# Query and key latents of an attention layer: eight-piece blocks alternated over half their depth, with the loads of x and the first vector work re-ordered

## The chip, the cores and the metric

The kernel runs on one NeuronCore of a Trainium2 chip. The metric is the device time of one execution in microseconds (us). Lower is better. The engines are named as in the profile: PE (TensorE matmul), PEld (its weight loads), DVE (VectorE), ACT (ScalarE), POOL (GpSimd), SP (SyncE, which issues most transfers).

## The reference, cut to what matters

A trunk of two layers over 256 tokens of width 2048: an attention mixer with low-rank ("latent") projections, a dense MLP, a Mamba-2 mixer, a dense MLP, each behind an RMSNorm and added to the residual stream, all in float32. The change sits in the first few tens of microseconds, in the first lines of the attention mixer:

```
h = rms_norm(x, mix_norm_g[0])                       # (256, 2048)
a = h @ w_in                                         # 2048 x (512 + 512 + 64)
c_q, c_kv, k_rope = split(a, [512, 1024])            # "q" latent, "c" latent, "r"
q  = (rms_norm(c_q,  q_norm_g)  @ w_uq ).reshape(B, S, 16, 192)
kv = (rms_norm(c_kv, kv_norm_g) @ w_ukv).reshape(B, S, 16, 256)
```

## The kernel before, in words

**Three passes per matmul.** Every float32 product is made of three passes in a reduced format: weights w are split into a high part `wh` (a copy on ACT, L102) and a remainder `wl` (a subtraction on DVE, L103), and so are activations (high and low tiles `xt`). High by high, low by high and high by remainder are added in one PSUM bank `acc`, one bank for each 128 tokens (t = 0, 1).

**Units.** Weights come in units of 128 x 1024 floats: two depth steps (k) of 128 by 512 columns, 512 KB. A unit costs PE 12 matmuls of 512 columns: 8 on `wh` (L339 and L340), then 4 on `wl` (L343). The depth of 2048 is 16 steps, so the q latent takes 8 units (called q0 to q7 here), the c latent 8 units (c0 to c7). Between them stands the 64-column `r` block (`narrow_block`, L358) as one unit. `sequence` writes down the order of all units. `Flow` loads a unit's raw tile (`wraw`, 6 buffers) up to 6 units ahead of the block that PE is at, and splits it up to 3 ahead into `wh` and `wl`, of which there are 4 buffers each. The unit numbered n therefore writes into the buffer of unit n-4 and waits until PE has read that. The numbers in names such as `wh14` are unit numbers. In both kernels the first 13 units are twelve latent units and the `r` block, `wh13` to `wh16` are the last four c units (c4 to c7), and `wh17` and `wh18` the two units of the block that follows (`uq`, 384 columns).

**Activations.** x comes transposed (`xT`) in four tiles `k` of four depth steps each, in eight transfers of one, two or four steps. `split_x` makes the high part (ACT, L480; the first on DVE, L478) and the low part (DVE, L481). The norm's factor is not applied to x: it is taken from row sums of squares of a second copy of x (`stats`, ACT L296, issued by `X_AT`), becomes `rs` on POOL (L283, L428), and scales the finished latents.

**Between blocks.** `latent` takes a finished latent through its own norm: squares on ACT (L296, with `rs` as scale), sums on DVE (L282), a power on POOL (L283), a product with `rs` (L811) and two scaled products on DVE (L816). The results are transposed on PE (L324) and split again (L299, L300). `later(n, fn)` puts a piece of work off by n+1 calls of `tick`, and `block` calls `tick` once for each key, so twice two units. `fold` (L366) finishes the `r` block.

**What sets the order.** PE's instructions run as written. The other engines' instructions are put in order by a scheduler at build time, and each engine then runs its own list strictly in that order. SP has its issues in such a list, too, and a transfer is issued when an earlier one of eight has landed.

Of the kernel before, what the change touches and what calls it, by code (L numbers as in the profile page):

```python
# [45 lines left out]
def inv_two_pi_parts():  # L46
    from fractions import Fraction
    pi = Fraction(3141592653589793238462643383279502884197169399375105820974944592307816406286, 10 ** 75)
    rest, parts = 1 / (2 * pi), []
    for _ in range(5):  # L50
        e = math.floor(math.log2(float(rest)))
        step = Fraction(2) ** (e - 11)
        part = (rest / step).__floor__() * step
        parts.append(float(part))
        rest -= part
    return parts
# [90 lines left out]
def classical(key, src, nk=4, n=512):  # L147

    def units(flow):
        out = []  # L150
        if n == 64:
            ld = Load("raw", src)
            return [Unit(key, nk, n, [ld], lambda: flow.narrow_halves(ld.tile))]
        for k in range(0, nk, 2):
            ld = Load("raw", src[:, k * n:(k + 2) * n])
            first = key == ("ain", "q", 0)
            out.append(Unit(key, 2, n, [ld], lambda ld=ld, f=first: flow.halves(ld.tile, 2 * n, 512 if f else None)))
        return out
    return units


def part(key, src):

    def units(flow):
        ld = Load("raw", src)
        return [Unit(key, 2, 512, [ld], lambda: flow.halves(ld.tile, 1024))]
    return units


# [45 lines left out]
class Trunk:  # L215
# [109 lines left out]
        self.split_out(h, lo, b.rearrange("p (k n) -> p k n", k=4))  # L325


    def block(self, keys, lhs, n=512, accs=None, first=True, last=True, mid=None):
        nc = self.nc
        if accs is None:  # L330
            accs = [self.acc_tile() for _ in range(2)]
        kt = 0
        for ik, key in enumerate(keys):
            for nk, wh, wl, end in self.flow.piece(key):
                en = last and ik == len(keys) - 1 and end
                for q in range(nk):
                    for t in range(2):
                        ah, al = lhs(kt + q, t)
                        nc.tensor.matmul(accs[t][:, :n], ah, wh[:, q, :], start=first and kt + q == 0, stop=False)  # L339
                        nc.tensor.matmul(accs[t][:, :n], al, wh[:, q, :], start=False, stop=False)  # L340
                for q in range(nk):
                    for t in range(2):
                        nc.tensor.matmul(accs[t][:, :n], lhs(kt + q, t)[0], wl[:, q, :], start=False, stop=en and q == nk - 1)  # L343
                kt += nk
                if mid and not end:
                    mid()
            self.tick()
        return accs

    def narrow_block(self, key, tiles, then, lag=1):  # L350
# [88 lines left out]
    def start(self, seq):  # L439
        nc, d = self.nc, self.d  # L440
        self.flow = Flow(nc, self.wp, seq, (6, 3))
        cst = self.c.tile([P, C_END], F32, name="cst")
        self.cst = cst
        self.ident_r = self.c.tile([P, P], F32R, name="ident")
        self.ident = self.ident_r.bitcast(F32)
        self.mhalf = self.c.tile([P, 16], F32, name="mhalf")
        warm = self.s2.tile([P, 512], F32R, tag="s2", name="warm")
        nc.vector.memset(warm.bitcast(F32), 1.0)
        bank = self.sm.tile([P, 512], F32, tag="sm", name="warmed")
        for _ in range(WARM):  # L450
            nc.tensor.matmul(bank, warm[:, :P], warm, start=True, stop=True)
        nc.gpsimd.memset(self.mhalf, -0.5)
        nc.scalar.dma_start(cst[:, C_G0:C_GQ], d["cst"][:, C_G0:C_GQ])
        nc.scalar.activation(self.stat(1), self.mhalf[:, :1], AF.Copy)
        raws = [self.ktile(self.k4, F32) for _ in range(4)]
        parts = [(0, slice(k, k + 1)) for k in range(4)] + [(1, slice(0, 2)), (1, slice(2, 4)), (2, slice(0, 4)), (3, slice(0, 4))]

        def some_x():
            j, k = parts.pop(0)
            nc.sync.dma_start(raws[j][:, k], d["xT"][j][:, k])  # L460

        self.flow.load(2, ((0, 512), (512, 1024)), some_x)
        for u in range(3, 7):
            some_x()
            self.flow.load(u)
        self.pos = self.c.tile([P, 2], I32, name="pos")
        self.x = [[self.res.tile([P, 512], F32, name=f"x{t}{n}") for n in range(4)] for t in range(2)]

        self.rs_pool = [self.c.tile([P, 4], F32, name=f"rs{i}") for i in range(2)]
        self.phase = 0  # L470
        self.xT = [(self.ktile(self.xtp), self.ktile(self.xtp)) for _ in range(4)]

        def split_x(j, ks):
            h, lo = self.xT[j]
            for k in ks:
                g = cst[:, C_G0 + 4 * j + k:C_G0 + 4 * j + k + 1]
                if (j, k) == (0, 0):
                    nc.vector.tensor_scalar(h[:, k], raws[j][:, k], g, None, ALU.mult)  # L478
                else:
                    nc.scalar.activation(h[:, k], raws[j][:, k], AF.Copy, scale=g)  # L480
                nc.vector.scalar_tensor_tensor(lo[:, k], raws[j][:, k], g, h[:, k].bitcast(F32), ALU.mult, ALU.subtract)  # L481

        split_x(0, (0,))
        self.flow.convert(1)
        split_x(0, (1, 2))
        self.flow.convert(2)
        split_x(0, (3,))
        self.flow.load(7)
        one = self.scratch()
        nc.sync.dma_start(one[:, :P], d["one"])  # L490
        nc.gpsimd.tensor_copy(self.ident_r, one[:, :P])
        nc.sync.dma_start(cst[:, C_GQ:], d["cst"][:, C_GQ:])
        nc.sync.dma_start(self.pos, d["pos"])
        split_x(1, range(4))
        ssq = self.stat(8)
        self.later(0, lambda: split_x(2, range(4)))
        self.later(1, lambda: split_x(3, range(4)))

        def stats(n):
            for t in range(2):  # L500
                nc.sync.dma_start(self.x[t][n], d["x"][t * P:(t + 1) * P, n * 512:(n + 1) * 512])
                self.square_sum(self.x[t][n], ssq[:, t * 4 + n:t * 4 + n + 1])
            if n == 3:
                self.set_rstd(ssq)

        for n, at in enumerate(X_AT):
            self.later(at, lambda n=n: stats(n))
# [318 lines left out]
    def mla_body(self, mp, gain):  # L826
        nc, d = self.nc, self.d
        cq = [mp.tile([P, 4, 256], F32R, name=f"cq{i}") for i in range(2)]
        ckv = [mp.tile([P, 4, 256], F32R, name=f"ckv{i}") for i in range(2)]
# [5 lines left out]
            self.rope_tables(mp)  # L835

        self.later(2, setup)
        xT = self.from_tiles(self.xT)
        accs = self.block([("ain", "q", q) for q in range(4)], xT)
        for fn in self.latent(accs, d["qg"], cq):  # L840
            self.later(3, fn)

        kro = mp.tile([P, 2, 64], F32, name="kro")
        krss = mp.tile([P, 4], F32, name="krss")
# [10 lines left out]
                nc.vector.tensor_tensor(kro[:, t], kraw[:, t], self.cst[:, C_GK + 128:C_GK + 192], ALU.mult)  # L855
            nc.vector.tensor_scalar(krss, krss, EPS, None, ALU.add)

        self.narrow_block(("ain", "r", 0), self.xT, k_rope, 3)
        accs = self.block([("ain", "c", q) for q in range(4)], xT)
        lat = self.latent(accs, d["kvg"], ckv, False)  # L860
        self.rope(mp, kro.unsqueeze(2))

        gq = self.cst[:, C_GQ:C_GQ + HD]
# [140 lines left out]
        lhs = self.from_tiles(oT)  # L1004
# [387 lines left out]
                self.boundary_end()  # L1392


X_AT = (1, 2, 3, 3)
HEAD_BACKLOG = 4
SSM_ORDER = ["B0", "d0", "C0", "x0", "B1", "x1", "C1", "x2", "z0", "x3", "z1", "x4", "z2", "o0", "x5", "z3", "x6", "z4", "o1",
             "x7", "z5", "z6", "o2a", "z7", "o2b", "o3"]
# [72 lines left out]
def sequence(d):  # L1471
    seq = []
    add = lambda *a: seq.append(classical(*a))
    for q in range(4):
        add(("ain", "q", q), d["ain"][q, 0])
    add(("ain", "r", 0), d["ainr"], 16, 64)
    for q in range(4):
        add(("ain", "c", q), d["ain"][q, 1])
    uq = lambda u: add(("uq", u), d["uq"][u], 4, 384)
    ukv = lambda u: add(("ukv", u), d["ukv"][u])  # L1480
    wo = lambda nb, qs: [add(("wo", q, nb), d["wo"][q, nb]) for q in qs]
# [31 lines left out]
    for step in SSM_ORDER:  # L1513
        kind, i = step[0], int(step[1])
# [16 lines left out]
def trunk(tc, d, out):  # L1531
    with ExitStack() as ctx:
        ctx.enter_context(tc.manual_schedule(engines={mybir.EngineType.PE}))
        k = Trunk(tc, ctx, d, out)
        k.start(sequence(d))
        k.mla(d["g"][0])
        k.mlp(0, d["g"][1])
        k.ssm(d["g"][2])
        k.mlp(1, None)
        k.drain()  # L1540
# [67 lines left out]
```

## Time and profile before

| what | value |
|---|---|
| time, median of 3 runs | 2286.64 us (2286.34 to 2287.26) |
| profiled execution, first to last instruction (span) | 2284.5 us |
| profiled execution's own time outside the span | not given; the median is 2.1 us above the span |
| PE busy | 2278.1 us, 100% of the span |
| DVE / ACT / POOL busy | 1915.9 / 1390.1 / 275.5 us |
| mean DMA rate over the span | 244 GB/s |

Lines of the timeline read: start in us, length in us, engine, source line, operation, output<-input, shape, and in brackets the idle time before it and what ended that. SPq and ACTq are issuing slots. Ends of matmuls are modelled, so the spacing of their starts is the safer number.

### The profile page before, as it was taken

How to read it: one execution, taken by the hardware profiler on the slowest of the kernel's cores; microseconds unless marked ns; L12 is line 12 of the kernel's file. 1: busy time of each engine (PE TensorE's matmuls, PEld its weight loads, DVE VectorE, ACT ScalarE, POOL GpSimd, SP SyncE). 2: the span in 40 equal slices, each digit the busy share in tenths (PEclk: the TensorE clock that was granted, in tenths of full speed). 3: DMA queues.
4: the chain of work that ended last, by engine and by line, in shares of the span. 5: the costliest groups of instructions: out<-in, count | busy, mean ns of one | idle time of the engine just before them, and what ended most of it. 6: DMA issues, size and time to landing. Idle time of an engine off the chain costs nothing.

```text
span 2284.5 us, 30768 instructions
## 1 busy us (share of the span) xinstructions
PE 2278.1 (100%) x10929; PEld 1889.6 (83%) x10929; DVE 1915.9 (84%) x2318; ACT 1390.1 (61%) x1947; POOL 275.5 (12%) x315
## 2 busy tenths in 40 slices
PE   9999999999999999999999999999999999999999
PEld 7898888888888888888888888888888888888887
DVE  7786698999898897687899688676989889989985
ACT  7775576566666666564666555545666666666663
POOL 1440000000000000100133213121000000000000
PEclk9999999999999999999999999999999999999999
DMA  8545678888888878667888787767688888888874
GB/s 315 173 153 159 211 230 267 259 255 270 264 255 259 267 232 271 227 208 241 277 280 278 245 275 264 229 222 229 204 265 248 259 270 253 260 275 247 267 232 160
DMA packets 167706, 557.16 MB, mean 244 GB/s; under 512 B 19040, under 2 KB 28192, under 8 KB 166528
## 3 DMA queue, kind: packets, MB, share of 16 engines
q1 hardware_dynamic: 151264, 502.44, 66.2%
q0 software_dynamic: 13888, 48.49, 10.0%
q10 hardware_dynamic: 2400, 4.27, 0.5%
q8 instruction: 86, 1.41, 0.3%
q14 instruction: 68, 0.56, 0.1%
HBM read 529.65 MB, written 6.41 MB: 235 GB/s over the span
## 4 chain that ended last, share of the span: by engine, by line
PE 96%; DVE 1%; DMA 1%; ACT 1%; issue 1%; POOL 0%; SPq 0%; ACTq 0%; DVEq 0%
PE acc L339 13%; PE acc L340 13%; PE acc L343 13%; PE yp L618 9%; PE yp L617 9%; PE yp L616 9%; PE st L617 7%; PE st L618 7%; PE st L616 7%; DMA wraw<-mi 1%; PE sm L324 1%; DVE wl L103 1%; PE y L1309 1%; PE sm L322 1%; PE acc L616 1%; PE acc L618 1%
## 5 line engine op out<-in xcount | busy, mean ns | idle before, releaser
L102 ACT ACTIVATE wh<-wraw 128x1024 fp32r<-128x1024 f32 (+1 forms) x818 | 856.2, 1053 | 570.4 <-PE acc L340 268.9
L103 DVE TENSOR_TENSOR wl<-wraw,wh 128x1024 fp32r<-128x1024 f32 (+1 forms) x818 | 985.5, 1221 | 240.6 <-ACT wh L102 216.6
L616 PE MATMUL yp<-wh,k 128*128 128x512 f32 x896 | 349.2, 390 | 0.0
L618 PE MATMUL yp<-wh,k 128*128 128x512 f32 x896 | 348.8, 389 | 0.0
L617 PE MATMUL yp<-wl,k 128*128 128x512 f32 x896 | 348.6, 389 | 0.0
L339 PE MATMUL acc<-wh,xt 128*128 128x512 f32 x704 | 279.7, 397 | 0.4 <-ACT wh L102 0.4
L340 PE MATMUL acc<-wh,xt 128*128 128x512 f32 x704 | 274.9, 390 | 0.1
L102 ACT ACTIVATE wh<-wrx 128x1024 fp32r<-128x1024 f32 x168 | 177.8, 1058 | 153.4 <-PE yp L618 101.7
L103 DVE TENSOR_TENSOR wl<-wrx,wh 128x1024 fp32r<-128x1024 f32 x168 | 204.3, 1221 | 36.6 <-ACT wh L102 35.6
L618 PEld LDWEIGHTS yp<-wh,k 128*128 128x128 f32 x896 | 168.2, 188 | 35.1
L617 PEld LDWEIGHTS yp<-wl,k 128*128 128x128 f32 x896 | 168.2, 188 | 34.9
L616 PEld LDWEIGHTS yp<-wh,k 128*128 128x128 f32 x896 | 168.2, 188 | 34.8
L339 PE MATMUL acc<-wh,k 128*128 128x512 f32 x496 | 196.5, 396 | 0.0
L340 PE MATMUL acc<-wh,k 128*128 128x512 f32 x496 | 193.3, 390 | 0.0
L343 PE MATMUL acc<-wl,xt 128*128 128x512 f32 x704 | 188.3, 389 | 0.0
L616 PE MATMUL st<-wh,xt 128*128 128x512 f32 x448 | 177.7, 397 | 0.0
L618 PE MATMUL st<-wh,xt 128*128 128x512 f32 x448 | 174.9, 390 | 0.0
L617 PE MATMUL st<-wl,xt 128*128 128x512 f32 x448 | 174.7, 390 | 0.0
L339 PEld LDWEIGHTS acc<-wh,xt 128*128 128x128 f32 x704 | 132.7, 188 | 29.4 <-ACT wh L102 1.6
L340 PEld LDWEIGHTS acc<-wh,xt 128*128 128x128 f32 x704 | 132.5, 188 | 28.5 <-issue 1.2
L343 PEld LDWEIGHTS acc<-wl,xt 128*128 128x128 f32 x704 | 132.1, 188 | 27.7
L199 POOL DMA_DIRECT2D wrx<-mi x56 | 49.2, 878 | 720.6 <-DVE wl L103 524.5
(318 smaller groups left out, 3527.0 us busy)
## 6 DMA issues: line engine op xcount, KB each, us to landing
wraw<-mi SPq DMA_DIRECT2D x256, 512.0 KB, 5.5
wraw<-mo SPq DMA_DIRECT2D x256, 512.0 KB, 5.6
wraw<-si SPq DMA_DIRECT2D x160, 512.0 KB, 5.2
wraw<-so SPq DMA_DIRECT2D x64, 512.0 KB, 5.2
wrx<-mi SPq DMA_DIRECT2D x56, 512.0 KB, 5.4
wrx<-mi POOLq DMA_DIRECT2D x56, 512.0 KB, 7.8
wraw<-wo SPq DMA_DIRECT2D x32, 512.0 KB, 4.0
taps<-xD SPq DMA_DIRECT2D x16, 768.0 KB, 8.4
```

The costliest lines, as they stand in the source:

```text
L102: self.last = nc.scalar.activation(h[:, v], raw[:, v], AF.Copy)
L103: self.last_lo = nc.vector.tensor_tensor(lo[:, v], raw[:, v], h[:, v].bitcast(F32), ALU.subtract)
L199: nc.gpsimd.dma_start(st["b11"].tile, quarter(d, 1, 0), accum_op=ALU.add)
L322: self.nc.tensor.transpose(b.bitcast(F32R)[:, v], words[:, v], self.ident_r)
L324: self.nc.tensor.transpose(b[:, v], src[:, v], self.ident)
L339: nc.tensor.matmul(accs[t][:, :n], ah, wh[:, q, :], start=first and kt + q == 0, stop=False)
L340: nc.tensor.matmul(accs[t][:, :n], al, wh[:, q, :], start=False, stop=False)
L343: nc.tensor.matmul(accs[t][:, :n], lhs(kt + q, t)[0], wl[:, q, :], start=False, stop=en and q == nk - 1)
L616: nc.tensor.matmul(b, ah, wh, start=first and q == 0, stop=False)
L617: nc.tensor.matmul(b, ah, wl, start=False, stop=False)
L618: nc.tensor.matmul(b, al, wh, start=False, stop=last and q == 1)
L1309: nc.tensor.matmul(y[t][c, o], part(t)[:, c], xg[g][t][:, o], start=True, stop=True)
```

## The change: what it does

- The 16 latent units are put in a new order: q0 c0 q1 c1 q2 c2 q3 c3, then q4 to q7, then the `r` block, then c4 to c7. Both latents hold their PSUM banks (4 in all) from the start. `tick` is called once per two units of one latent.
- Since two latents share each x tile in the first half, x's tile 1 is loaded between weights, and tiles 2 and 3 after seven units of weights.
- Within a unit the two token halves alternate: high t0, high t1, low t0, low t1, where it was high t0, low t0, high t1, low t1.
- DVE's first instructions are put in written order: both first low parts of x before the first weight remainder `wl0`.
- The q latent's transposes are put off by 1 instead of 3, the `r` block's `fold` by 2 instead of 3, and `X_AT` moves the last piece of `stats` one tick on.

```diff
-            first = key == ("ain", "q", 0)
-            out.append(Unit(key, 2, n, [ld], lambda ld=ld, f=first: flow.halves(ld.tile, 2 * n, 512 if f else None)))
+            out.append(Unit(key, 2, n, [ld], lambda ld=ld: flow.halves(ld.tile, 2 * n)))
...
-def part(key, src):
+def part(key, src, step=None):
...
-        return [Unit(key, 2, 512, [ld], lambda: flow.halves(ld.tile, 1024))]
+        return [Unit(key, 2, 512, [ld], lambda: flow.halves(ld.tile, 1024, step))]
...
-    def block(self, keys, lhs, n=512, accs=None, first=True, last=True, mid=None):
+    def block(self, keys, lhs, n=512, accs=None, first=True, last=True, mid=None, tick=True):
...
-                    for t in range(2):
-                        ah, al = lhs(kt + q, t)
-                        nc.tensor.matmul(accs[t][:, :n], ah, wh[:, q, :], start=first and kt + q == 0, stop=False)
-                        nc.tensor.matmul(accs[t][:, :n], al, wh[:, q, :], start=False, stop=False)
+                    for part in range(2):
+                        for t in range(2):
+                            nc.tensor.matmul(accs[t][:, :n], lhs(kt + q, t)[part], wh[:, q, :],
+                                             start=first and kt + q + part == 0, stop=False)
...
-            self.tick()
+            if tick:
+                self.tick()
...
-        for u in range(3, 7):
+        for u in (4, 6):
+            self.flow.load(u)
             some_x()
-            self.flow.load(u)
...
-        split_x(0, (0,))
-        self.flow.convert(1)
-        split_x(0, (1, 2))
+        with self.tc.manual_schedule(engines={mybir.EngineType.DVE}):
+            split_x(0, (0, 1))
+            self.flow.convert(1)
         self.flow.convert(2)
-        split_x(0, (3,))
+        split_x(0, (2, 3))
         self.flow.load(7)
+        some_x()
+        some_x()
...
-        xT = self.from_tiles(self.xT)
-        accs = self.block([("ain", "q", q) for q in range(4)], xT)
-        for fn in self.latent(accs, d["qg"], cq):
-            self.later(3, fn)
+        lat = {n: [self.acc_tile() for _ in range(2)] for n in "qc"}
+
+        def latents(steps):
+            for n, i in steps:
+                self.block([("ain", n, i)], self.from_tiles(self.xT, 2 * i), accs=lat[n], first=i == 0, last=i == 7, tick=i % 2)
+
+        latents(LATENTS[:12])
+        for fn in self.latent(lat["q"], d["qg"], cq):
+            self.later(1, fn)
...
-        self.narrow_block(("ain", "r", 0), self.xT, k_rope, 3)
-        accs = self.block([("ain", "c", q) for q in range(4)], xT)
-        lat = self.latent(accs, d["kvg"], ckv, False)
+        self.narrow_block(("ain", "r", 0), self.xT, k_rope, 2)
+        latents(LATENTS[12:])
+        lat = self.latent(lat["c"], d["kvg"], ckv, False)
...
-X_AT = (1, 2, 3, 3)
+X_AT = (1, 2, 3, 4)
+LATENTS = [(n, i) for i in range(4) for n in "qc"] + [("q", i) for i in range(4, 8)] + [("c", i) for i in range(4, 8)]
```

Three places where the order of instructions moves. In the names, `wraw` and `wh` are raw and high weights, `k` the raw tiles of xT, `xt` split x, `acc_16` and `acc_17` the q latent's banks, `s2` scratch tiles, `cq` the transposed q latent.

SP's issues before, from the second half of the second unit (`wraw_124`) on. Names such as `k_3` are x tiles: `k_2` is x's first tile.

```order
L85 DMA wraw_124<-ain 128x512
L460 DMA k_2_115<-xT 128x256
L460 DMA k_3_116<-xT 128x512
L85 DMA wraw_130<-ain 128x1024
L460 DMA k_3_116<-xT 128x512
L85 DMA wraw_133<-ain 128x1024
L460 DMA k_4_117<-xT 128x1024
L85 DMA wraw_136<-ain 128x1024
L460 DMA k_5_118<-xT 128x1024
```

The same place in the changed kernel:

```order
L85 DMA wraw_124<-ain 128x512
L460 DMA k_2_115<-xT 128x256
L85 DMA wraw_129<-ain 128x1024
L85 DMA wraw_131<-ain 128x1024
L460 DMA k_3_116<-xT 128x512
L85 DMA wraw_134<-ain 128x1024
L85 DMA wraw_136<-ain 128x1024
L460 DMA k_3_116<-xT 128x512
L85 DMA wraw_181<-ain 128x1024
L460 DMA k_4_117<-xT 128x1024
L460 DMA k_5_118<-xT 128x1024
```

The third unit's weights moved ahead of a half of x's second tile; x's last two tiles (`k_4`, `k_5`) moved behind three and four more units.

ACT's list around the q latent's squares, before. `s2_31` and `s2_32` are the squares of `acc_16` and `acc_17`.

```order
L102 ACTIVATE wh14_545<-wraw14_464 128x1024
L102 ACTIVATE wh15_563<-wraw15_507 128x1024
L296 ACTIVATE s2_31_443,st_30_442<-acc_16_204,rs0_150 128x512
L296 ACTIVATE s2_32_445,st_30_442<-acc_17_205,rs0_150 128x512
L777 ACT_TABLE_LOAD
L777 ACTIVATE angp_361<-angs_360 128x64
L778 ACTIVATE angp_361<-angs_360 128x64
L102 ACTIVATE wh16_593<-wraw16_525 128x1024
L102 ACTIVATE wh17_611<-wraw17_543 128x768
L102 ACTIVATE wh18_659<-wraw18_561 128x768
L299 ACTIVATE cq0_199<-sm_43_627 128x4x128
```

And in the changed kernel, where the squares write `s2_33` and `s2_34`:

```order
L102 ACTIVATE wh16_596<-wraw16_483 128x1024
L102 ACTIVATE wh17_614<-wraw17_501 128x768
L102 ACTIVATE wh18_646<-wraw18_541 128x768
L295 ACTIVATE s2_33_520,st_32_519<-acc_16_207,rs0_148 128x512
L295 ACTIVATE s2_34_522,st_32_519<-acc_17_208,rs0_148 128x512
L298 ACTIVATE cq0_202<-sm_43_630 128x4x128
L298 ACTIVATE cq0_202<-yp_44_637 128x4x128
```

The squares moved from ahead of the splits `wh16` to `wh18` to behind them.

PE's list at the q latent's transposes, before: the end of unit `wh14`, the transposes, the fold, the next unit.

```order
L340 MATMUL acc_42_506<-wh14_545,xt_11_157 128x512
L343 MATMUL acc_41_505<-wl14_546,xt_10_156 128x512
L343 MATMUL acc_42_506<-wl14_546,xt_10_156 128x512
L343 MATMUL acc_41_505<-wl14_546,xt_10_156 128x512
L343 MATMUL acc_42_506<-wl14_546,xt_10_156 128x512
L324 MATMUL sm_43_627<-ident_97,s2_37_455 128x128 x4
L324 MATMUL yp_44_634<-ident_97,s2_38_457 128x128 x4
L366 MATMUL sm_45_641<-cst_96,s2_40_503 128x64 x2
L339 MATMUL acc_41_505<-wh15_563,xt_12_158 128x512
```

And in the changed kernel:

```order
L338 MATMUL acc_19_210<-wh14_503,xt_11_155 128x512
L342 MATMUL acc_18_209<-wl14_504,xt_10_154 128x512
L342 MATMUL acc_19_210<-wl14_504,xt_10_154 128x512
L342 MATMUL acc_18_209<-wl14_504,xt_10_154 128x512
L342 MATMUL acc_19_210<-wl14_504,xt_10_154 128x512
L323 MATMUL sm_43_630<-ident_97,s2_39_532 128x128 x4
L323 MATMUL yp_44_637<-ident_97,s2_40_534 128x128 x4
L338 MATMUL acc_18_209<-wh15_543,xt_12_156 128x512
```

The transposes stand behind the same unit in both; the fold moved from here to behind unit `wh16`. Between the q latent's last matmul and these transposes stood the `r` block and six c units before; now the `r` block and two.

More of the change, by code (lines that the diff above doesn't have):

```diff
@@ L1473, in sequence @@
     add = lambda *a: seq.append(classical(*a))
[L1474 to L1478, printed above, removed]
+    for j, (n, i) in enumerate(LATENTS):
+        if j == 12:
+            add(("ain", "r", 0), d["ainr"], 16, 64)
+        seq.append(part(("ain", n, i), d["ain"][i // 2, "qc".index(n)][:, (i % 2) * 1024:(i % 2) * 1024 + 1024], 512 if j < 2 else None))
     uq = lambda u: add(("uq", u), d["uq"][u], 4, 384)
```

## The prediction

> **What bounds the kernel.** I read the page's busy times and the chain first, then the stages of the first 100 us, then the timeline of each engine there.
>
> ```profile
> PE 2278.1 (100%) x10929; PEld 1889.6 (83%) x10929; DVE 1915.9 (84%) x2318; ACT 1390.1 (61%) x1947; POOL 275.5 (12%) x315
> PE 96%; DVE 1%; DMA 1%; ACT 1%; issue 1%; POOL 0%; SPq 0%; ACTq 0%; DVEq 0%
> core 0: 2284.5 us, clock 1.000
> ```
>
> PE idles for 2284.5 - 2278.1 = 6.4 us in all. A change that keeps PE's work can only remove part of that, or add to it. Behind the first 73 us the lists of all engines are the same in both kernels but for names and line numbers, so the early stretch decides. In the stages below the columns are length, then busy time and count for PE, PEld, DVE, ACT, POOL, then clock, DMA share and GB/s.
>
> ```profile
> 5.45:9.40 3.95, 3.81 (x13) 2.75 (x13) 3.02 (x7) 2.88 (x6) 0.00 (x0) 1.00 0.91 273
> 9.40:12.67 3.27, 2.90 (x13) 2.00 (x11) 1.86 (x5) 2.26 (x5) 0.00 (x0) 1.00 1.02 402
> 12.67:15.53 2.86, 2.86 (x12) 2.36 (x13) 2.86 (x4) 2.56 (x5) 0.00 (x0) 1.00 1.02 418
> ...
> 1.45 4.21 PE L451 MATMUL warmed<-warm 128*128 128x512 f32 x9 [1.45 <-DVE warm L448]
> 5.45 0.63 PE L339 MATMUL acc<-wh,xt 128*128 128x512 f32 x1
> 6.22 0.79 PE L340 MATMUL acc<-wh,xt 128*128 128x512 f32 x1
> 7.24 0.50 PE L340 MATMUL acc<-wh,xt 128*128 128x512 f32 x1
> 7.58 0.40 PE L339 MATMUL acc<-wh,xt 128*128 128x512 f32 x1
> 12.67 0.50 PE L339 MATMUL acc<-wh,xt 128*128 128x512 f32 x1 [0.37 <-ACT wh L102]
> 15.53 0.39 PE L339 MATMUL acc<-wh,xt 128*128 128x512 f32 x1
> 18.25 0.39 PE L339 MATMUL acc<-wh,xt 128*128 128x512 f32 x1
> ```
>
> A unit in step takes 18.25 - 15.53 = 2.72 us; the first three took 3.95, 3.27 and 2.86, so 1.92 us above three such units. In step, starts are 2.72/12 = 0.23 apart. Part of the excess is slow matmuls: the warm-up ones are (5.45 - 1.45)/9 = 0.44 apart, and from 7.24 to 7.58 it is still 0.34. Part is waiting: 0.77 from 5.45 to 6.22 (x's low part), and the wait before the third unit.
>
> **Start: alternating units, x later, remainder behind x.** PE's second matmul is now the other token half's high part, at about 5.45 + 0.44 = 5.89; the low part is needed third, at 6.33. DVE makes it right behind the first high part, so before 6.0:
>
> ```profile
> 5.08 0.68 DVE L103 TENSOR_TENSOR wl<-wraw,wh 128x512 fp32r<-128x512 f32 x1
> 5.69 0.48 DVE L481 SCALAR_TENSOR_TENSOR xt<-k,cst,xt 128x256 fp32r<-128x256 f32 x1
> 5.91 0.49 ACT L480 ACTIVATE xt<-k,cst 128x256 fp32r<-128x256 f32 x1
> 11.56 1.06 ACT L102 ACTIVATE wh<-wraw 128x1024 fp32r<-128x1024 f32 x1 [0.51 <-DMA wraw<-ain]
> 14.79 1.71 ACT L480 ACTIVATE xt<-k,cst 128x256 fp32r<-128x256 f32 x4 [0.22 <-DMA k<-xT]
> ```
>
> x's second step is ready on ACT at 6.40 and its low part near 6.95; both remainders follow by 6.95 + 2 x 0.68 = 8.31. PE needs the first of them eight starts behind 5.45: four at 0.44, one at 0.34, three at 0.23, or 8.24. So the first unit ends near 8.31 + 4 x 0.23 = 9.2, for 9.4 in the first row above. The second (c0) uses the same two steps of x, so it runs in step to 11.9, where before q1 needed x's third and fourth step. The third needs its weights, which landed at 11.54 with 256 KB of x ahead of them. At 402 GB/s those cost 0.65 us, so they land near 10.9 and are split by 11.95. The third unit starts at about 12.0 and the fourth at 14.73 for 15.53: **gain 0.8 us**. Bounds: nothing, if the weights land no sooner; 1.9, the whole excess. I take 0.8, which follows the rows. Moving x's tiles 2 and 3 back costs nothing: tile 2 was split at 14.79, and even four units of 512 KB more ahead of it are 4 x 1.3 = 5.2 us at 402 GB/s, while PE wants it at the ninth unit, 14.73 + 5 x 2.72 = 28.3. The pairing of token halves leaves the matmul count alone; zero.
>
> **The wait that is added.** The q latent's squares stand behind `wh18` on ACT. That split writes the buffer of `wh14`, so it waits until PE has read unit c5, and PE's next instructions after c5 are the transposes that need those squares. Before, the same split waited at the same place, with the squares long done:
>
> ```profile
> 41.41 0.67 ACT L296 ACTIVATE s<-acc,rs 128x512 f32<-128x512 f32 x1
> 48.60 0.85 ACT L102 ACTIVATE wh<-wraw 128x768 fp32r<-128x768 f32 x1 [1.82 <-PE acc L340]
> ...
> 48.18 0.39 PE L340 MATMUL acc<-wh,xt 128*128 128x512 f32 x1
> 48.41 1.07 PE L343 MATMUL acc<-wl,xt 128*128 128x512 f32 x4
> 49.32 0.60 PE L324 MATMUL sm<-ident,s 128*128 128x128 f32 x4
> 49.75 0.60 PE L324 MATMUL yp<-ident,s 128*128 128x128 f32 x4
> 50.19 0.56 PE L366 MATMUL sm<-cst,s 128*128 128x64 f32 x4
> 50.55 0.48 PE L339 MATMUL acc<-wh,xt 128*128 128x512 f32 x1
> ```
>
> Let H be the start of that split. PE would reach the transposes at H + 49.32 - 48.60 = H + 0.72 and, as the fold has left this place, the next unit at H + 50.19 - 48.60 = H + 1.59. The chain's price is read off the c latent, which has the same steps behind an equal split:
>
> ```profile
> 55.47 0.85 ACT L102 ACTIVATE wh<-wraw 128x768 fp32r<-128x768 f32 x1 [0.98 <-ACT s L296]
> 56.22 0.67 ACT L296 ACTIVATE s<-acc,rs 128x512 f32<-128x512 f32 x1
> ...
> 57.68 0.17 DVE L282 TENSOR_SCALAR st<-st 128x2 f32<-128x2 f32 x1 [0.34 <-ACT s L296]
> 57.93 0.72 POOL L283 TENSOR_TENSOR st<-st,mhalf 128x2 f32<-128x2 f32 x1 [3.11 <-DVE st L282]
> 58.69 0.16 DVE L811 TENSOR_TENSOR st<-st,rs 128x2 f32<-128x2 f32 x1 [0.84 <-POOL st L283]
> 58.88 1.41 DVE L816 SCALAR_TENSOR_TENSOR s<-acc,st,gb 128x512 f32<-128x512 f32 x2
> ```
>
> Split to squares 0.75; squares to the end of the first product 58.88 + 0.70 - 56.22 = 3.36, of the second 58.88 + 1.41 - 56.22 = 4.07. With 0.05 to PE (5.69 + 0.48 to 6.22), the transposes start at H + 4.16 and H + 4.87, and the next unit at 4.87 + 0.44 = H + 5.31. **Cost 5.31 - 1.59 = 3.7 us.** Bounds: 3.0, were the split free; about 5, if DVE, which has `wl18` (0.95) ahead of the sums, also delays them. That remainder is done near H + 1.9 and the squares near H + 2.2, so it should not. The factor `rs` is not what is late: before, it took from 37.81 to 40.37 + 0.53 = 40.90 from the last square of x to the factor, 3.1 us:
>
> ```profile
> 42.86 1.28 ACT L777 ACT_TABLE_LOAD   x1
> 37.81 0.62 ACT L296 ACTIVATE s<-x 128x512 f32<-128x512 f32 x1
> 40.37 0.53 POOL L428 COPY rs<-st 128x2 f32<-128x2 f32 x1
> ```
>
> The last two squares now stand behind `wh15`, whose buffer is read at 14.73 + 8 x 2.72 + 8 x 0.23 = 38.3, with the table load between them: 38.3 + 1.06 + 0.7 + 1.28 + 0.4 + 3.1, about 45, against H near 48.60 - 0.8 = 47.8. What is queued behind `wh18` are only these squares; DMA issues on SP go on, as raw buffers are freed by DVE's remainders of earlier units.
>
> **Behind it.** The fold (0.36) is moved, not removed: zero. It now opens the `uq` block, and its four small squares on ACT and POOL's rotation stand ahead of the c latent's chain, some 2 us; that chain had finished at 60.29, while PE reached its transposes at 62.40, so its 2.1 us of cover are about used up. Next comes PE's one wait there:
>
> ```profile
> 62.40 1.03 PE L324 MATMUL sm<-ident,s 128*128 128x128 f32 x8
> 67.78 1.39 POOL L798 TENSOR_TENSOR ra<-qn,cc 128x256 f32<-128x256 f32 x1 [4.08 <-DVE qn L887]
> 70.74 1.89 DVE L887 SCALAR_TENSOR_TENSOR qn<-yp,st,cst 128x128 f32<-128x128 f32 x8 [2.17 <-POOL st L290]
> 71.88 0.63 PE L939 MATMUL yp<-ident,qn 128*128 128x128 f32 x4 [0.41 <-DVE qn L887]
> ```
>
> The transposes need the `yp` bank that these products read. They wait for a root on POOL, which stood behind the rotation's first piece (1.39) before and now stands ahead of it; PE comes 0.36 later by the fold. That is 1.7 us in favour, for a wait of 0.41. So the 0.41 goes: **gain 0.4 us**, bounds 0.4 and -1, if the late c chain pushes the same products back.
>
> **Sum.** 3.7 - 0.8 - 0.4 = +2.5 us. The profiled span becomes 2287.0; what lies outside it (2.1 us to the median, which is all the runs tell of it) is untouched, so 2286.64 + 2.5 = 2289.1.
>
> **A rule that speaks against it.** PE stands still from H + 0.88 (48.41 + 1.07) to H + 4.16, 3.3 us, with only transposes until H + 5.31. No gap in this trace is that long, so no row shows whether PE's matmuls are slow again behind it, as they were up to 7.3 us. The Trainium skill, "TensorE: Matmul & The Clock Gate", "Part 1: The HAM clock gate", says an idle window of about 3.4 us halves PE's clock until a like window of work; one such slow window would add an estimated 3.4 x (1 - 0.23/0.44) = 1.6 us, giving 2290.7. The granted clock cannot settle it: the column reads 1.00 during the slow start too.
>
> **Rivals.**
> - *PE comes back slow (0.17).* From rows: slow starts ran from 1.45 to about 7.3, 5.8 us at 0.44 for 0.23, or 2.8 us lost. At most 2289.1 + 2.8 = 2291.9, at least a little over 2289.1. For it: the length of the stop. Against: 3.3 us is short of the 5.8 that the start took.
> - *No new wait, so faster (0.08).* If PE's stop at the transposes is under 1.2 us, the two gains decide; without any stop 2286.64 - 1.2 = 2285.4. That needs the squares to run while `wh18` waits. ACT's list speaks against it, and in the trace ACT's work behind such a split started only as it ended (55.47, then 56.22).
> - *The start gains nothing (0.10).* Weights land as late as before; then 2289.9. For it: DMA share is 1.02 throughout. Against: 256 KB less lie ahead.
> - *A second wait at the late c chain (0.12).* Up to 1 us more at the `uq` block's transposes and 0.4 not gained: 2290.5.
>
> **How the numbers follow.** The forecast holds 0.53. A change within 0.2% (4.57 us), about what a measurement here can tell from none, reaches to 2291.2. The slow return passes that in perhaps half of its cases, a double wait in some: slower 0.12. Nothing in 6.4 us of idle time makes 4.57 us likely: faster 0.01. The range takes in the start's bounds, the second wait and half of the slow return: 2287.6 to 2291.6.
>
> **What would show it.** Right: PE's idle time at L323's first transposes near 48.5 us, about 3.3 us, released by DVE L818; the fourth unit at about 14.7; no wait at the first `qn` transposes. Wrong: squares (L295 on `acc`) ahead of the last 768-column split's start, or matmuls 0.44 apart behind the stop.

## The result, and the profile after

The changed kernel took 2289.71 us (median of 21 runs, 2286.49 to 2291.14), the kernel before 2286.22 (21 runs, 2285.41 to 2288.19). The ratio is 1.0015, 95% interval 1.0009 to 1.0021: 3.5 us slower, within the 0.2% called no difference above. The profiled execution spans 2287.7 us, 3.2 more than before.

The page's busy times and the clock of the core, after:

```profile
PE 2278.2 (100%) x10929; PEld 1890.0 (83%) x10929; DVE 1916.4 (84%) x2318; ACT 1390.2 (61%) x1947; POOL 270.9 (12%) x315
core 0: 2287.7 us, clock 0.999
```

PE's count is the same. Its sum of busy time moved by 0.1 only, though matmuls ran slow for a while: 1.5 us more from the transposes to the end of c6's high products stand against 0.7 less up to the fourth unit, 0.4 less on the first `ckv` unit and some tenths elsewhere. The sum hides all of that; the starts show it. The timeline of PE after, in four stretches (high products are now L338, products with remainders L342, transposes L323; one row is a run of equal instructions):

```profile
4.97 1.17 PE L338 MATMUL acc<-wh,xt 128*128 128x512 f32 x4
8.79 2.09 PE L338 MATMUL acc<-wh,xt 128*128 128x512 f32 x8
12.02 2.11 PE L338 MATMUL acc<-wh,xt 128*128 128x512 f32 x8 [0.22 <-ACT wh L102]
14.87 1.30 PE L338 MATMUL acc<-wh,xt 128*128 128x512 f32 x5
...
47.74 1.07 PE L342 MATMUL acc<-wl,xt 128*128 128x512 f32 x4
52.26 1.08 PE L323 MATMUL sm<-ident,s 128*128 128x128 f32 x4 [3.45 <-DVE s L818]
53.14 1.06 PE L323 MATMUL yp<-ident,s 128*128 128x128 f32 x4
53.85 2.90 PE L338 MATMUL acc<-wh,xt 128*128 128x512 f32 x8
56.59 1.09 PE L342 MATMUL acc<-wl,xt 128*128 128x512 f32 x4
...
69.92 2.01 PE L338 MATMUL acc<-wh,ckv 128*128 128x512 f32 x8
72.68 1.98 PE L338 MATMUL acc<-wh,ckv 128*128 128x512 f32 x8
75.40 0.60 PE L946 MATMUL yp<-ident,qn 128*128 128x128 f32 x4
75.97 1.66 PE L338 MATMUL acc<-wh,cq 128*128 128x384 f32 x8
```

The answering rows of before that were not shown yet, from the same view of PE:

```profile
52.49 1.08 PE L343 MATMUL acc<-wl,xt 128*128 128x512 f32 x4
65.35 0.40 PE L339 MATMUL acc<-wh,ckv 128*128 128x512 f32 x1
65.81 0.50 PE L340 MATMUL acc<-wh,ckv 128*128 128x512 f32 x1
68.59 0.39 PE L339 MATMUL acc<-wh,ckv 128*128 128x512 f32 x1
72.48 0.42 PE L339 MATMUL acc<-wh,cq 128*128 128x384 f32 x1
```

PE runs its list in order, so the difference of starts between equal points is a ledger:

| stretch on PE | before | after | difference |
|---|---|---|---|
| to the start H of `wh18`'s split | 48.60 | 47.94 | -0.66 |
| H to the first matmul of unit c6 (before, the fold's 0.36, which both kernels pay once, is left out) | 1.59 | 5.91 | +4.32 |
| c6's eight high products | 1.94 | 2.74 | +0.80 |
| c6's low products to the first unit on `ckv` (before, with the fold's 0.36 put in) | 13.22 | 13.33 | +0.11 |
| first unit on `ckv` | 3.24 | 2.76 | -0.48 |
| second unit on `ckv` to the first `qn` transposes | 3.29 | 2.72 | -0.57 |
| sum | | | +3.52 |

At the next block's first product PE is 75.97 - 72.48 = 3.49 late; the medians differ by 3.49. That the two agree so closely is chance: behind this point single executions differ by more. The run e1 below stands 0.57 us ahead of the kernel before here (71.91), and its span is still 1.5 us longer (2286.0).

The stop is 3.45 us long and ended by DVE L818, the latent's scaled product. The chain ahead of it, from the timelines of ACT, DVE and POOL after:

```profile
47.94 0.85 ACT L102 ACTIVATE wh<-wraw 128x768 fp32r<-128x768 f32 x1 [1.82 <-PE acc L338]
48.70 0.67 ACT L295 ACTIVATE s<-acc,rs 128x512 f32<-128x512 f32 x1
50.16 0.17 DVE L281 TENSOR_SCALAR st<-st 128x2 f32<-128x2 f32 x1 [0.29 <-ACT s L295]
50.41 0.73 POOL L282 TENSOR_TENSOR st<-st,mhalf 128x2 f32<-128x2 f32 x1 [4.10 <-DVE st L281]
51.37 1.41 DVE L818 SCALAR_TENSOR_TENSOR s<-acc,st,gb 128x512 f32<-128x512 f32 x2
45.07 0.18 POOL L428 COPY rs<-st 128x2 f32<-128x2 f32 x1
```

ACT waits 1.82 us in front of `wh18` with the squares queued behind it. Their factor `rs` was there at 45.25, so it was the order of ACT's list and no late input that held them.

Behind the stop the matmuls are slow, and the windows of 1 us after (columns as above) show it in the granted clock, the third figure from the right:

```profile
51.00:52.00 1.00, 0.00 (x0) 0.00 (x0) 0.79 (x2) 0.00 (x0) 0.14 (x1) 1.00 0.83 215
52.00:53.00 1.00, 0.74 (x4) 0.77 (x5) 1.00 (x3) 0.00 (x0) 0.00 (x0) 0.59 0.37 148
53.00:54.00 1.00, 1.00 (x7) 1.00 (x5) 0.10 (x1) 0.60 (x1) 0.00 (x0) 0.50 0.41 49
54.00:55.00 1.00, 1.00 (x4) 0.81 (x4) 0.82 (x2) 0.60 (x1) 0.00 (x0) 0.50 0.64 211
55.00:56.00 1.00, 1.00 (x5) 0.81 (x4) 0.56 (x1) 0.00 (x0) 0.00 (x0) 0.71 0.08 16
56.00:57.00 1.00, 1.00 (x6) 0.83 (x5) 0.00 (x0) 0.21 (x1) 0.00 (x0) 1.00 0.01 2
```

If a reading of 0.59 means a part of the window at half, the time at half is 0.82 + 1 + 1 + 0.58 = 3.4 us. The core's mean clock, 0.999 against 1.000, is the same thing seen from far off: 3.4 x 0.5 of 2288 us is 0.07%. Of the 21 executions 17 read 0.999 (median 2290.27) and four 1.000 (2286.49 to 2288.86, median 2287.6). The 2.7 us between these medians are no price of the slow window: there are only four, and the executions of the kernel before lie 2.8 us apart by themselves. The mean clock is printed to 0.001, so a stretch at half clock of less than about 2.3 us (0.0005 x 2288 / 0.5) would still read 1.000.

### The profile page after: what moved, and what is told of

Its sections match the earlier page's. It is cut to its first block, busy times and chain, and to the rows that moved or that the text cites. A ratio compares the mean times of both kernels' runs of the same rounds, so it can differ in the third digit from the quotient of the medians.

```text
span 2287.7 us, 30764 instructions
## 1 busy us (share of the span) xinstructions
PE 2278.2 (100%) x10929; PEld 1890.0 (83%) x10929; DVE 1916.4 (84%) x2318; ACT 1390.2 (61%) x1947; POOL 270.9 (12%) x315
## 4 chain that ended last, share of the span: by engine, by line
PE 96%; DMA 1%; DVE 1%; ACT 1%; issue 0%; POOL 0%; SPq 0%; ACTq 0%; DVEq 0%
PE acc L338 26%; PE acc L342 13%; PE yp L618 9%; PE yp L619 9%; PE yp L620 9%; PE st L619 7%; PE st L620 7%; PE st L618 7%; PE sm L323 1%; PE y L1316 1%; PE sm L321 1%; PE acc L620 1%; PE acc L619 1%; PE acc L618 1%; DMA wraw<-mi 1%; DVE wl L103 0%
## 5 line engine op out<-in xcount | busy, mean ns | idle before, releaser
L338 PE MATMUL acc<-wh,xt 128*128 128x512 f32 x1408 | 355.0, 394 | 0.6 <-ACT xt L480 0.4
L338 PEld LDWEIGHTS acc<-wh,xt 128*128 128x128 f32 x1408 | 262.3, 188 | 58.1 <-issue 2.1
L338 PE MATMUL acc<-wh,k 128*128 128x512 f32 x992 | 248.9, 393 | 0.0
L338 PEld LDWEIGHTS acc<-wh,k 128*128 128x128 f32 x992 | 185.0, 188 | 39.1 <-issue 1.2
L342 PE MATMUL acc<-wl,xt 128*128 128x512 f32 x704 | 188.6, 390 | 0.0
L342 PEld LDWEIGHTS acc<-wl,xt 128*128 128x128 f32 x704 | 132.0, 188 | 28.2 <-DVE wl L103 0.6
L618 PE MATMUL st<-wh,sN 128*128 128x512 f32 x336 | 133.0, 396 | 0.0
L342 PE MATMUL acc<-wl,k 128*128 128x512 f32 x496 | 132.7, 389 | 0.0
```

The lines of the kernel that those rows point to most:

```text
L338: nc.tensor.matmul(accs[t][:, :n], lhs(kt + q, t)[part], wh[:, q, :], start=first and kt + q + part == 0, stop=False)
L618: nc.tensor.matmul(b, ah, wh, start=first and q == 0, stop=False)
```

## Experiments

Each compares with the kernel before on the same chip. The theory: PE's stop comes from the list order on ACT, and a slow window comes on top of it. The rivals: the factor `rs`, the fold's or the `uq` block's new place carries the loss, or the stop alone does and the clock is a bystander. Where a kernel has one line more near its top, the same instructions stand at L339, L343 and L324.

**e1: the squares ahead of `wh18`.** The changed kernel, with one dependency more for the scheduler.

```diff
-        self.nc.scalar.activation(junk[:, :n], src, AF.Square, scale=scale, accum_out=acc)
+        self.squared = self.nc.scalar.activation(junk[:, :n], src, AF.Square, scale=scale, accum_out=acc)
...
+            with self.after() if self.done == 18 else nullcontext():
+                self.last = nc.scalar.activation(h[:, v], raw[:, v], AF.Copy)
...
+        squared = self.squared
+        self.flow.after = lambda: self.tc.issue_after(squared.ins)
```

> The changed kernel with one edge added: the split of unit wh18 on ACT may only follow the q latent's squares. Theory (the squares stand behind a split that waits for PE): rs is ready at 45.25 and wh17 starts at 45.27, so the squares run from 46.0, the first product ends at 46.0 + 3.4 = 49.4, and PE's stop before the transposes shrinks from 3.45 to about 0.8 us, with no matmuls at half clock behind it. Time: the changed kernel less 2.6 for the stop and less 1.5 for the slow window, about 4 us, so 0.5 to 1 us below the kernel before. Rival (the factor rs or the sums are late whatever ACT's order): stop and time unchanged, 3.5 us above before.

Measured: 2285.72 us (11 runs, 2284.18 to 2287.81) against 2286.08 (33 runs), ratio 0.9997, 0.9988 to 1.0005; mean clock 1.000 in all eleven. PE's timeline at the same place:

```profile
49.65 0.63 PE L324 MATMUL sm<-ident,s 128*128 128x128 f32 x4 [0.78 <-DVE s L819]
50.62 2.10 PE L339 MATMUL acc<-wh,xt 128*128 128x512 f32 x8
52.56 1.08 PE L343 MATMUL acc<-wl,xt 128*128 128x512 f32 x4
```

The stop shrinks from 3.45 to 0.78 us, c6's eight high products take 1.94 again, and the time is back. The order of these entries on ACT carries the whole loss: 3.49 + 0.36 = 3.85 us between the medians. The expectation held in the stop and the clock; the time is 0.36 us below before, where 0.5 to 1 was written, and the interval allows both. On DVE the remainder of `wh18` moved behind the products with it; in the changed kernel that remainder was done before the sums could start (they still waited 0.29 us for ACT), so it held nothing up.

**e2: the stop filled with matmuls.** Thirteen products whose result is not used, ahead of the transposes; the chain keeps its place.

```diff
+        fill_x = self.xT[3][0]
+        def fill():
+            b = self.yp.tile([P, 512], F32, tag="yp", name=self.name("fill"))
+            for i in range(13):
+                nc.tensor.matmul(b, fill_x[:, i % 4, :P], fill_x[:, 0:2, :], start=True, stop=True)
+        self.later(1, fill)
```

> The changed kernel with 13 matmuls of 512 columns on split x, into a bank nobody reads, put ahead of the q latent's transposes (added work, 13 x 0.23 = 3.0 us, inside PE's stop). Theory (an idle PE loses its clock for one window): the stop's end stays where it is, the clock reads 1.00 behind it, transposes and the next unit run in step, and the time falls by 1.5 to 1.7 us against the changed kernel, to about 1.9 us above before. Rival (the slow matmuls come from the transposes or from something else that happens there): they stay slow and the time stays 3.5 us above before, or rises if the added work outlasts the stop.

Measured: 2288.61 us (11 runs, 2287.11 to 2290.7) against 2286.08, ratio 1.0011, 1.0002 to 1.002; mean clock 1.000 in all eleven. PE's timeline:

```profile
49.06 3.11 PE L852 MATMUL fill<-xt 128*128 128x512 f32 x13
52.67 0.63 PE L323 MATMUL sm<-ident,s 128*128 128x128 f32 x4 [0.51 <-DVE s L818]
53.65 2.09 PE L338 MATMUL acc<-wh,xt 128*128 128x512 f32 x8
55.58 1.07 PE L342 MATMUL acc<-wl,xt 128*128 128x512 f32 x4
```

The transposes still wait for the same product, so the useful work is held as long. But from them to c6 it is 0.98 us and not 1.59, and c6's eight take 1.93 and not 2.74: 0.61 + 0.81 = 1.4 us that the idle time cost beyond itself. The rival that the transposes themselves bring the slow matmuls is out. In the medians the gain over the changed kernel is 3.5 - 2.5 = 1.0 us, less than the 1.5 to 1.7 expected; the interval of this run is 2 us wide to either side, so the 1.4 read in place is the better figure.

**e5 and e6: three and seven matmuls.** As e2, with one number changed, to see how long PE has to idle.

```diff
-            for i in range(13):
+            for i in range(3):
```

> The changed kernel with 3 added matmuls (0.7 us) ahead of the q latent's transposes: PE's stop stays, but only about 2.75 us of it are idle. If the clock is halved only when a whole window of about 3.4 us is idle, all executions keep a mean clock of 1.000 and the time is that of the run with 13 (2.5 us above before). If a mostly idle window is enough, the slow window stays in a good part of the executions (mean clock 0.999) and the median lies between 2.5 and 3.5 us above before.

```diff
-            for i in range(13):
+            for i in range(7):
```

> The same with 7 added matmuls (1.6 us), so about 1.85 us idle. Both theories: clock 1.000 and 2.5 us above before; slow windows here would mean that half a window of idle time is enough.

Measured against 2286.25 (33 runs): three, 2289.32 us (11 runs, 2287.56 to 2290.83), ratio 1.0014, 1.0005 to 1.0023; seven, 2288.95 (11 runs, 2287.76 to 2290.12), ratio 1.0011, 1.0002 to 1.002. PE's timeline with three and the window behind, then with seven:

```profile
52.25 0.64 PE L323 MATMUL sm<-ident,s 128*128 128x128 f32 x4 [2.77 <-DVE s L818]
53.58 3.28 PE L338 MATMUL acc<-wh,xt 128*128 128x512 f32 x8
...
53.00:54.00 1.00, 1.00 (x5) 1.00 (x5) 0.54 (x2) 0.55 (x2) 0.00 (x0) 0.50 0.46 59
```

```profile
52.43 0.63 PE L323 MATMUL sm<-ident,s 128*128 128x128 f32 x4 [1.86 <-DVE s L818]
53.41 2.10 PE L338 MATMUL acc<-wh,xt 128*128 128x512 f32 x8
```

With the idle time of the profiled execution beside it, the executions with a mean clock of 0.999 are: 3.45 us, 17 of 21; 2.77 us, 8 of 11; 1.86 us, 2 of 11; 0.51 us (e2) and 0.78 us (e1), none of 11 each. In e5 the three executions at 1.000 are its three fastest (2287.56, 2287.62 and 2288.38). In e6 the two at 0.999 (2289.04 and 2289.26) are not its slowest. So a whole idle window of 3.4 us is not needed, as e5 was to show, and at seven matmuls, where no slow execution was expected, two came. None of the 66 executions of the kernel before that were measured beside e1 to e8 reads 0.999.

**e3: the squares ahead of `wh17`.** As e1, one split earlier.

```diff
-            with self.after() if self.done == 18 else nullcontext():
+            with self.after() if self.done == 17 else nullcontext():
```

> The same edge one split earlier: wh17 and wh18 both follow the q latent's squares. Theory: squares from 45.3, first product at 48.7, just when PE gets there, so no stop over 0.2 us; the gains at the start (0.7) and at the qn wait (0.4) stand alone: 1.1 us below the kernel before, 4.6 below the changed one. Rival (splitting wh17 and its remainder later starves PE at the uq block): a new wait at the first uq matmuls, time between the changed kernel and before.

Measured: 2284.95 us (11 runs, 2283.29 to 2286.17) against 2286.08, ratio 0.9992, 0.9983 to 1.0001. By the modelled ends PE goes from c5's last products (47.68 + 1.07 = 48.75) into the transposes, and into those of `qn`, without a wait. By the starts a little is left: the transposes begin 48.81 - 47.68 = 1.13 behind these products, where 0.91 (48.41 to 49.32 before) is in step:

```profile
48.81 0.63 PE L324 MATMUL sm<-ident,s 128*128 128x128 f32 x4
49.79 2.10 PE L339 MATMUL acc<-wh,xt 128*128 128x512 f32 x8
70.50 0.60 PE L949 MATMUL yp<-ident,qn 128*128 128x128 f32 x4
```

The fold stands in its new place here too, and no loss is seen there. With the stop gone, the change is worth about -1.1 us, near the sum that the prediction gave for "no new wait" (-1.2), though 0.48 of the gain come at `ckv`, which that sum did not hold. The interval just reaches 1, so the gain is likely and not shown.

**e7: e3 with the row sums of x one tick earlier**, to see whether `rs` still holds anything.

```diff
-X_AT = (1, 2, 3, 4)
+X_AT = (1, 2, 3, 3)
```

> The run with the squares ahead of wh17, with x's sums of squares one tick earlier as well (X_AT 1, 2, 3, 3), so that the factor rs comes earlier than 45. Theory: the last 0.2 us of PE's stop go too; 1.2 to 1.4 us below before. If rs was not what the squares waited for, no change against the run without it (1.1 below).

Measured: 2285.15 us (11 runs, 2283.9 to 2287.13) against 2286.25, ratio 0.9996, 0.9987 to 1.0005. The medians of e3 and e7 are the same, but they cannot show some tenths. The traces can. First e3's squares and e7's, then e7's transposes and next unit:

```profile
45.22 0.69 ACT L296 ACTIVATE s<-acc,rs 128x512 f32<-128x512 f32 x1 [1.69 <-POOL rs L429]
43.47 0.69 ACT L296 ACTIVATE s<-acc,rs 128x512 f32<-128x512 f32 x1 [0.37 <-POOL rs L429]
...
48.65 0.60 PE L324 MATMUL sm<-ident,s 128*128 128x128 f32 x4
49.44 2.07 PE L339 MATMUL acc<-wh,xt 128*128 128x512 f32 x8
```

In e3 the squares waited for `rs`; in e7 they run 1.75 us earlier, the transposes begin in step (48.65 - 47.74 = 0.91 behind c5's low products), and c6 begins 49.44 - 47.74 = 1.70 behind them, where e3 has 49.79 - 47.68 = 2.11. So the factor held up e3 by 0.4 us, as the theory said; with the order on ACT right, `rs` is the next thing in line.

**e4: blocks alternate over a quarter of the depth.** The q latent then ends two units earlier, with more room for its chain.

```diff
-        latents(LATENTS[:12])
+        latents(LATENTS[:10])
...
-            self.later(1, fn)
+            self.later(2, fn)
...
-X_AT = (1, 2, 3, 4)
-LATENTS = [(n, i) for i in range(4) for n in "qc"] + [("q", i) for i in range(4, 8)] + [("c", i) for i in range(4, 8)]
+X_AT = (1, 2, 3, 3)
+LATENTS = [(n, i) for i in range(2) for n in "qc"] + [("q", i) for i in range(2, 8)] + [("c", i) for i in range(2, 8)]
```

> The units alternate over a quarter of the depth only (q0 c0 q1 c1, then q2 to q7, r, c2 to c7), the transposes 3 ticks on, x's sums of squares one tick earlier (X_AT 1, 2, 3, 3). The squares then stand right behind wh14 on ACT. Theory: no stop, the start's gain kept (its first three units are the same): 0.7 to 1.1 us below before. Rival (the gain at the start needs the longer alternation, because x's tiles 2 and 3 come late): a wait at the seventh or ninth unit, and no gain.

Measured: 2286.04 us (11 runs, 2284.66 to 2287.25) against 2286.08, ratio 0.9999, 0.999 to 1.0008. PE's timeline:

```profile
12.64 2.11 PE L338 MATMUL acc<-wh,xt 128*128 128x512 f32 x8 [0.73 <-ACT wh L102]
49.28 0.60 PE L323 MATMUL sm<-ident,s 128*128 128x128 f32 x4
71.83 0.63 PE L946 MATMUL yp<-ident,qn 128*128 128x128 f32 x4 [0.39 <-DVE qn L894]
```

No stop, but no gain either: the third unit waited 0.73 us for its weights and the `qn` transposes 0.39. The first `ckv` unit is as slow as before, too (65.32 to 68.55). So the gains at `qn` and `ckv` are no gift of alternation as such; they hang on what the lists look like there. In this run the fold stands beside the transposes again, as before.

**e8: e3 with the old order of loads.** x's tiles come between the weights as before.

```diff
-        for u in (4, 6):
+        for u in range(3, 7):
-            self.flow.load(u)
             some_x()
+            self.flow.load(u)
...
-        some_x()
-        some_x()
```

> The run with the squares ahead of wh17, with the loads of x and weights in the order of before (a part of x's second tile ahead of the third unit's weights, tiles 2 and 3 between the next ones). Theory (the start's gain needs the weights earlier): the third unit starts 0.4 to 0.7 us later than there (11.95), at 12.3 to 12.7, behind a wait for its high part, and half or more of the gain at the start is lost. Rival (order of loads does not matter, pairing and remainder make the gain): third unit by 12.1.

Measured: 2286.26 us (11 runs, 2284.34 to 2287.62) against 2286.25, ratio 1.0000, 0.9991 to 1.0009. The third unit starts at 12.49, behind a wait of 0.60, where e3 has 11.95 without one:

```profile
12.49 2.12 PE L339 MATMUL acc<-wh,xt 128*128 128x512 f32 x8 [0.60 <-ACT wh L103]
11.95 2.12 PE L339 MATMUL acc<-wh,xt 128*128 128x512 f32 x8
```

The split of the third unit's weights, which waits for their landing, starts at 11.38 here, as with the old loads of e12 (11.37), and at 10.83 in e3. So the later loads of x are the likely source of the start's gain. It is one profile, and e4 with the new loads had to wait until 11.53; the medians, known to 2 us either way, cannot decide it.

**e10 and e11: the other two edits at the start, undone one at a time in e3.** One execution each.

```diff
-        with self.tc.manual_schedule(engines={mybir.EngineType.DVE}):
-            split_x(0, (0, 1))
-            self.flow.convert(1)
+        split_x(0, (0,))
+        self.flow.convert(1)
+        split_x(0, (1, 2))
...
-            split_x(0, (2, 3))
+            split_x(0, (3,))
```

> The run with the squares ahead of wh17, with DVE's first instructions as before (half of the first remainder ahead of x's first low part, half ahead of the second). Theory: the third matmul, which needs the low part, waits until 6.2 instead of running at 6.3, so the order alone is worth at most 0.2 us: second unit at 9.1 to 9.3.

```diff
-                    for part in range(2):
-                        for t in range(2):
+                    for t in range(2):
+                        for part in range(2):
```

> The same, with the token halves in the order of before (high, low of half 0, then of half 1) and DVE's new order. Theory: the second matmul needs x's low part, which is done by 5.7 now, so little waits: second unit at 9.1 to 9.3. If pairing is what makes the gain, the second unit starts at 9.4 as before.

Measured: 2284.65 and 2285.95 us, against 2286.55 (the kernel before, once). With DVE's old order the second unit starts at 8.92 and the fourth at 14.82, as in e3 (9.13 and 14.80). Unpaired, the second starts at 9.22 and the fourth at 14.66. Neither edit is worth anything at the fourth unit that one execution can show. (e10 also had a wait of 0.56 us at the q latent's transposes, which e3 had not.)

**e9 and e12: the kernel before, profiled again**, to see how far its start varies by itself. No edit.

> The kernel before, profiled once more, to see how much its first units vary from one execution to another. If the loads land alike each time, units start at 5.45, 9.4, 12.7 and 15.5 again; if they vary as in the changed kernels (third unit 11.95 to 12.64), by some tenths.

> The kernel before, unchanged, profiled once more. If the start's gain of the change is a matter of the loads' order alone, the units of products start within 0.1 us of the first profile of before (third 12.67, fourth 15.53 us) and the chain's place is the same: squares from 47.08, transposes without a stop. If the first landings vary from run to run, the third and fourth unit start up to 0.7 us earlier or later by the wait for their weights, and the 0.66 us by which the changed kernel stood ahead is not all the change's. Time between 2285.4 and 2288.2 us either way.

e9 took 7028.17 us once, with a granted clock of 1.00 and matmuls of 512 columns 0.84 us apart for most of it (0.62 near its end); nothing else is read from it and its cause is open. e12 took 2287.18 us; its third unit starts at 12.48 and its fourth at 15.35, 0.18 ahead of the first profile. Fourth units start at 15.53, 15.35 and 15.35 with the old loads (before, e12, e8), and from 14.66 to 15.50, mean 14.96, in the ten profiles with the new ones. The start's gain is then 0.45 us in the mean. The 0.66 of the first comparison holds some luck, and the luck is in the landing: with the same first loads the split of the third unit's weights started at 10.91 in the changed kernel, 11.27 in e2 and 11.53 in e4, and the unit 1.11 later each time. When the first matmul came is not what counts: 4.97 in the changed kernel and 5.45 in e7, with the fourth unit at 14.87 in both.

## Why the prediction was right, and where not

Its time, 2289.1 us, was 0.6 below the median; the sum of +2.5 stands against +3.5. That the time is the nearer of the two is luck: it was added to a median of three, 2286.64, and the 21 runs of the kernel before have 2286.22. By its steps:

- **The added wait: right, in place, releaser and size.** Squares at H + 0.76 (0.75 forecast), first transposes at H + 4.32 (4.16), a stop of 3.45 us (3.3) ended by DVE L818. The factor came at 45.25 ("about 45"). e1 shows the cause by moving the squares alone.
- **The clock behind it: the step that failed.** The sum took matmuls in step behind the stop and left the slow return to a rival at 0.17. It came in 17 of 21 executions (0.50 in the granted clock, c6's high products in 2.74 us for 1.94) and cost 1.4 us by e2. The argument against it used the wrong neighbour: how long the slow start lasts says nothing of how long an idle time brings one on. The claim that the granted clock cannot settle it was wrong too; it reads 0.50 here. The size given beside it was good: the rule of the Trainium skill, "TensorE: Matmul & The Clock Gate", "Part 1: The HAM clock gate", gave an estimated 1.6 us. Its window of about 3.4 us agrees with the 3.4 us at half clock here. Its bound on the idle time does not quite: 2.77 us were enough in 8 of 11 executions, 1.86 in 2 of 11.
- **The start: right in kind, too large.** 0.66 us in the one comparison and 0.45 in the mean over profiles, for 0.8. The weights landed at 10.91 as forecast (10.9):

```profile
10.91 1.06 ACT L102 ACTIVATE wh<-wraw 128x1024 fp32r<-128x1024 f32 x1 [0.87 <-DMA wraw<-ain]
```

  The third unit began at 12.02, as forecast (12.0), but took 2.85 us, as before (2.86), where the sum had 2.72: that is what is missing in the one comparison. The mean is smaller still because the old loads of e12 and e8 also did better than the first profile of before (15.35 for 15.53) and some of the new ones did worse. e8 puts the gain on the loads, by one profile. The story told of the first unit (the low part and the remainders in step) bought little: undone in e10 and e11, the fourth unit starts the same.
- **Behind it: right at `qn`, blind at `ckv`.** The `qn` wait went, for 0.57 us (0.4 forecast). PE's first unit on `ckv` also got 0.48 us faster, which no step held: its first matmuls were 0.46 apart before (65.35 to 65.81) where 0.23 is in step, and the eight take 72.68 - 69.92 - 0.91 = 1.85 after. DVE's list shows why, before and then after:

```profile
65.07 1.28 DVE L300 TENSOR_TENSOR ckv<-sm,ckv 128x512 fp32r<-128x512 f32 x2
68.89 1.28 DVE L299 TENSOR_TENSOR ckv<-sm,ckv 128x512 fp32r<-128x512 f32 x2
```

  Before, `ckv`'s low parts stood behind two `qn` products and a remainder (63.74 to 65.15) and PE's second matmul waited for them; after, they stand ahead of both and start 1.0 us before PE gets there. No run moves this entry alone. But all ten profiles in which the fold stands behind c7 have 2.76 us and no wait at `qn`, among them those without the paired halves (e11), the new loads (e8) and the new order on DVE (e10); the three in which it stands beside the transposes (before, e12, e4) have 3.23 or 3.24 and the wait. So the fold's new place is the likely cause. The second wait at the late c chain did not come, by little: its products were done at 66.71 and PE took them at 66.93.
- **The sum's errors partly cancel**: +0.14 (start), +0.60 and +0.80 (c6 reached late, mostly by slow transposes, then slow), +0.11 (c6 to `ckv`), -0.48 (`ckv`), -0.17 (`qn`), together +1.0.

## What to carry to other kernels

When work moves along an engine's list, ask of every entry put in front of it what that entry waits for: here a split that waited for PE held up squares that PE itself was waiting for, and one dependency at build time took 3.85 us off. Price a stop of PE of nearly 3 us or more at its length plus a slow return in most executions (1.4 us here), and look for it in the granted clock of 1 us windows, not in busy sums. Before a gain of half a microsecond at a kernel's start is put down to an edit, take several profiles: the start varies about as much by itself.

## What the runs showed of the hardware

- An idle PE loses its clock at no sharp length: 17 of 21 executions at 3.45 us, 8 of 11 at 2.77, 2 of 11 at 1.86, none at 0.5 to 0.8. A chance that grows with the length fits these counts better than one threshold; what decides a single execution the runs do not show.
- Behind the stop the granted clock reads 0.50 for about 3.4 us. During the slow start of the kernel it reads 1.00 while matmuls are 0.44 apart, so in this case a low reading went with slow matmuls, but a reading of 1.00 did not rule them out.
- The same loads do not bring the same start: the third unit began between 11.94 and 12.64 us in the ten profiles with the new loads, the latest (e4) behind a wait of 0.73 for its split weights, which had landed 0.6 us later than in the changed kernel (11.53 for 10.91).
